# Output projection: two pairs of token tiles per pass instead of one

## The chip, the cores and the metric

The kernel runs on one core of a Trainium2 chip. The metric is the time of one execution on the device in microseconds (us); the median of three runs before is 1721.08 us (1716.45 to 1728.96). Engines are named as in the profile: PE (matrix products), PEld (loading of its stationary operand), DVE (VectorE), ACT (ScalarE), POOL (GpSimd) and SP (here it only issues transfers). Each engine works through its own list in order.

## The reference, cut to what matters

One layer over 2048 tokens of 1024 features: modulated RMSNorm, one input projection, a pooling group and a gated recurrence with 8 heads ("the mixers"), and an output projection. Only the last part matters here:

```python
y = jnp.concatenate([pool_out, hgrn_out], axis=-1) @ w_out[l]     # (2048, 2048) @ (2048, 1024)
h_res = h_res + gate * rms_norm(y, norm_post_w[l])
```

Both mixer groups give 1024 of the 2048 columns that enter `w_out`. All is float32; a product of two float32 matrices is made of three passes in a rounded format (hi times hi, hi times lo, lo times hi), where `lo` is the value less its rounded `hi` (`part`, lines 127 to 130: a copy on ACT, a subtraction on DVE).

## The kernel before, in words

Up to about 1356 us the mixers run. They write their outputs to a buffer `mix` in HBM, and W_out's Strassen sums to `wos`. Then comes the output projection, which is all that the change touches.

It does a matrix product in Strassen-Winograd form: 7 products instead of 8 for a 2x2 block product. Its loop (lines 923 to 966) has 16 steps, called granules here: for g = 0 (the pooling group's half of W_out) and then g = 1 (the recurrence's half), 8 pairs `p_` of token tiles of 128 tokens. One granule works as follows.

- `mix_granule` (lines 819 to 845) loads the two tiles (two transfers of 512 KB, line 823) into the single buffer `raw`, forms on POOL the sums S1, S2, S3, S4 (lines 834, 837, 838, 842: four operations on 128x512) and splits each of seven operands by `part` (lines 129, 130) into a tile `m`, one of six buffers of the tag "w". It is called for the next granule before the products of this one.
- `quad` (lines 376 to 407) makes the seven products A11, S1, S2, A12, S3, S4, A22. Each product is 12 matmuls of 128x128 by 128x512 (line 373). Three PSUM banks X, Z, Y take them: A11 and A12 go into X, S1 and S4 into Z, S2, S3 and A22 into Y. Products add up in a bank, and between two that use the same bank its content is read: line 395 reads Y after S2, line 400 after S3, line 403 Z after S4, line 406 Y after A22, line 389 Z after S1 (all on DVE), line 381 and line 940 X (ACT). So the product that is next in a bank waits for a reader on DVE: S2 into Y and S3 into Y have one other product between them (A12), S3 and A22 too (S4).
- For g = 0 the two result tiles `y` (buffers "y", four) go to HBM as `ypart` (line 945). For g = 1 `ypart` is loaded again (line 936) and added (DVE, line 952, four operations per granule), the sum of squares is taken (ACT, line 957), a power on POOL gives the factor (lines 111, 112), DVE scales (line 961, four), x is loaded (line 954) and added on POOL (line 962, four; in the last granule on DVE), and the tile is stored (line 966; in the last granule in halves, line 964).
- `ypart`, x and the raw pieces of W_out (`load_out`, lines 794 to 817: 14 pieces of 512 KB, each split by `part` or lines 811, 812 into S-tiles that all granules of one g share) use one ring of five buffers, tag "px". `load_out` runs at the start of each g; 28 S-tiles hold one g.

The memory comes from pools that are opened and closed like a stack. `ws` (working tiles of the recurrence) is closed before the last pooling step, and `fin` with "px" and "y" takes its place. `wsp` holds the rest of the mixers' small tiles, `og`, `vc`, `hx` and others (made by `short`, line 138), until the end. The last mixer step is `pool_step` for kb = 7; its two `pool_block` calls (lines 532 to 561) end in a DVE multiplication (line 560) and a store of `sg` to `mix` (line 530).

The order on each engine and queue is laid out ahead by a planner that simulates the times: at each point it takes what is ready, earlier code first, and code in `tc.high_priority()` before that. `load_out(0)` and the first `mix_granule` stand in the code before the last `pool_step`.

Of the kernel before, what the change touches and what calls it, by code (L numbers as in the profile page):

```python
# [44 lines left out]
def build(nc, tc, a):  # L45
# [6 lines left out]
    with tc.tile_pool(name="dram", bufs=1, space=DRAM) as dram, \  # L52
# [21 lines left out]
        def raw_tile(name, shape, dt=F32):  # L74
            return big.tile(shape, dt, name=name, tag="raw", bufs=1)
# [56 lines left out]

        wsp_cm = tc.tile_pool(name="wsp", bufs=1)
        wsp = wsp_cm.__enter__()
        ws_cm = tc.tile_pool(name="ws", bufs=1)
        ws = ws_cm.__enter__()

        def short(name, tag, bufs=1, n=BLK, pool=None):
            return (pool or wsp).tile([P, n], F32, name=name, tag=tag, bufs=bufs)


        masks = {0: cp.tile([P, 32], U8, name="mask0"), 1: cp.tile([P, 16], U8, name="mask1")}
        for q in range(4):
# [3 lines left out]
        mt = wsp.tile([P, 64], F32, name="mt", tag="hx", bufs=2)  # L147
        for m in (2, 4, 8, 16):
            n = 64 // m
            mv = mt.rearrange("p (n m) -> p n m", m=m)  # L150
# [57 lines left out]

        ct = cp.tile([P, KB], F32, name="ct")
        load(ct, a["c"][0].rearrange("(p j) -> p j", j=KB))  # L210
        rows = wsp.tile([P, P], F32, name="rows", tag="w0", bufs=2)
# [164 lines left out]
        def quad(W, c12, c21, c22, begin=None, out=False):  # L376

            X, Z, Y = bank("mm"), bank("mm"), bank("mm")
            product(X, W[0], S["A11"], True)
            with tc.high_priority():  # L380
                nc.scalar.copy(c21, X)
            if begin:

                product(X, W[3], S["A12"], False)
                begin()
            product(Z, W[1], S["S1"], True)
            with tc.high_priority():
                if out:
                    nc.vector.tensor_tensor(c22, Z, c21, ALU.add)
                else:  # L390
                    nc.scalar.copy(c22, Z)  # L391
                    nc.gpsimd.tensor_tensor(c22, c22, c21, ALU.add)  # L392
# [99 lines left out]
        def gate_row():  # L492
# [2 lines left out]
            got = []  # L495

            def fetch(j, n):
                t_ = short("adag", "junk")
# [319 lines left out]

        def mix_granule(g, p_):

            raw = raw_tile("mraw", [P, 2, KB, P])
            for i in range(2):
                nc.sync.dma_start(raw[:, i], mix[2 * p_ + i][:, g * KB:(g + 1) * KB])
            A11, A12, A21, A22 = (raw[:, i, h * KH:(h + 1) * KH] for i in range(2) for h in range(2))
            S1 = wsp.tile([P, KH, P], F32, name="S1", tag="hx", bufs=2)

            def put(src):
                w = w_tile("m")
                wv = w.rearrange("p s (k n) -> p s k n", n=P)
                part(wv[:, 0], wv[:, 1], src)  # L830
                return wv

            r = [put(A11)]
            nc.gpsimd.tensor_tensor(S1, A21, A22, ALU.add)  # L834
            r.append(put(S1))

            nc.gpsimd.tensor_tensor(S1, S1, A11, ALU.subtract)
            nc.gpsimd.tensor_tensor(A21, A11, A21, ALU.subtract)
            r.append(put(S1))
            r.append(put(A12))  # L840
            r.append(put(A21))
            nc.gpsimd.tensor_tensor(S1, A12, S1, ALU.subtract)
            r.append(put(S1))
            r.append(put(A22))
            return r


        steps = []
# [40 lines left out]
        for i, step in enumerate(steps):  # L889
# [3 lines left out]
                load_sums()  # L893
            nxt = weights(steps[i + 1]) if 0 < i < len(steps) - 1 else None
            if i == len(steps) - 1:
                nxt = mix_granule(0, 0)
                O = load_out(0)
            if half == 0 and (what == "hv" and n < HEADS - 1 or what == "pool" and n == HEADS - 1):
                beside(second_sums(n), 2)
# [20 lines left out]
                fin_cm = tc.tile_pool(name="fin", bufs=1)  # L920
                fin.append(fin_cm.__enter__())

        todo = [(g, p_) for g in range(2) for p_ in range(T // P // 2)]
        M = nxt
        for i, (g, p_) in enumerate(todo):
            if p_ == 0:
                S.update(load_out(1) if g else O)
            if g and p_ == 0:
                gn = wsp.tile([P, D], F32, name="gnb", tag="x1", bufs=1)
                nc.sync.dma_start(gn, gnrow[0].partition_broadcast(P))  # L930
            nxt = mix_granule(*todo[i + 1]) if i + 1 < len(todo) else None
            y = [fin[0].tile([P, D], F32, name="y", tag="y", bufs=4) for _ in range(2)]
            if g:
                parts = [fin[0].tile([P, D], F32, name="yp", tag="px", bufs=5) for _ in range(2)]
                for t in range(2):
                    nc.sync.dma_start(parts[t], ypart[2 * p_ + t])
            X = quad(M, y[0][:, BLK:], y[1][:, 0:BLK], y[1][:, BLK:], out=True)
            M = nxt
            with tc.high_priority():
                nc.scalar.copy(y[0][:, 0:BLK], X)  # L940
            if g == 0:
                for f in out_sums(1, p_ % 4, p_ // 4):
                    f()
                for t in range(2):
                    nc.sync.dma_start(ypart[2 * p_ + t], y[t])
                continue
            final = i == len(todo) - 1
            for t in range(2):
                ts = slice((2 * p_ + t) * P, (2 * p_ + t + 1) * P)
                for n in (t, 1 - t):  # L950
                    ns = slice(n * BLK, (n + 1) * BLK)
                    nc.vector.tensor_tensor(y[t][:, ns], y[t][:, ns], parts[t][:, ns], ALU.add)
                xt = fin[0].tile([P, D], F32, name="xf", tag="px", bufs=5)
                nc.sync.dma_start(xt, x[ts])
                ss = wsp.tile([P, 1], F32, name="ss1", tag="ss1", bufs=2)
                junk = wsp.tile([P, D], BF16, name="junk", tag="junk", bufs=1)
                nc.scalar.activation(junk, y[t], AF.Square, accum_out=ss)
                rstd_of(ss, 1, 1.0 / D)
                for n in range(2):
                    ns = slice(n * BLK, (n + 1) * BLK)  # L960
                    nc.vector.scalar_tensor_tensor(y[t][:, ns], y[t][:, ns], ss, gn[:, ns], ALU.mult, ALU.mult)  # L961
                    (nc.vector if final else nc.gpsimd).tensor_tensor(y[t][:, ns], y[t][:, ns], xt[:, ns], ALU.add)
                    if final:
                        nc.sync.dma_start(out[ts, ns], y[t][:, ns])
                if not final:
                    nc.sync.dma_start(out[ts], y[t])
        fin_cm.__exit__(None, None, None)
        wsp_cm.__exit__(None, None, None)

# [15 lines left out]
```

## Time and profile before

| what | value |
|---|---|
| median of the runs | 1721.08 us (1716.45 to 1728.96) |
| the profiled execution's own time | 1724.97 us |
| its span | 1723.3 us |
| PE busy | 1599.1 us, 93% |
| DVE busy | 1101.9 us, 64% |
| POOL busy | 694.5 us, 40% |
| ACT busy | 638.3 us, 37% |
| PE with line 373 in the chain that ended last | 38% of the span |
| DMA in that chain | 17% |

The span is the time from the first to the last instruction of one profiled execution; the time of that execution lies 1.7 us above it. A matmul's busy time runs to its modelled end, and matmuls overlap, so PE's share looks fuller than the work is; a stretch is best judged by how many matmuls it holds. Shares are averages over stages with different limits.

### The profile page before, as it was taken

What the parts mean: (1) busy time and instruction counts of PE and PEld (TensorE: products, weight loads), DVE (VectorE), ACT (ScalarE), POOL (GpSimd) and SP (SyncE); (2) the same over time, 40 slices, a digit from 0 to 9 for tenths busy, and PEclk for the clock granted to TensorE, in tenths of its full rate; (3) what the DMA queues carried; (4) which work ended last, traced back from release to release, by engine and by line L of the source; (5) the groups of instructions that cost most, each with busy time, mean ns of one, the idle gap of its engine ahead of it and who ended that gap; (6) DMA issues with size and microseconds to landing.
All of it is one profiled execution on the core that took longest, in us unless ns stands there. A gap on an engine that the chain in (4) does not pass through costs nothing.

```text
span 1723.3 us, 31604 instructions
## 1 busy us (share of the span) xinstructions
PE 1599.1 (93%) x12249; PEld 1278.4 (74%) x12249; DVE 1101.9 (64%) x1763; ACT 638.3 (37%) x1409; POOL 694.5 (40%) x915
## 2 busy tenths in 40 slices
PE   7679999999999999889999999889999899989896
PEld 6557787887877777767788787677888678867775
DVE  5587767586676868765553545353555864587886
ACT  4554344444444453342223132323222432353332
POOL 1375454746455565211221243534021233225664
PEclk8789999999999999999999999999999999999999
DMA  9637476766757676885344567666545652285553
GB/s 358 228 114 241 174 247 205 243 216 221 231 191 233 215 240 195 292 289 182 120 142 163 179 201 229 214 231 216 204 156 171 208 196 110 98 268 171 192 182 128
DMA packets 221476, 348.67 MB, mean 202 GB/s; under 512 B 45009, under 2 KB 152590, under 8 KB 221326
## 3 DMA queue, kind: packets, MB, share of 16 engines
q1 hardware_dynamic: 221240, 346.62, 59.9%
q8 instruction: 97, 1.59, 0.4%
q14 instruction: 53, 0.43, 0.1%
q10 hardware_dynamic: 86, 0.03, 0.0%
HBM read 203.99 MB, written 142.61 MB: 201 GB/s over the span
## 4 chain that ended last, share of the span: by engine, by line
PE 47%; DMA 17%; DVE 12%; POOL 10%; issue 7%; ACT 4%; SPq 1%; POOLq 0%; DVEq 0%; ACTq 0%
PE ps_mm L373 38%; DMA x<-w_out 4%; DMA wraw<-w_in 3%; DMA wos<-x 3%; DVE m L130 2%; DVE w L130 2%; PE ps_lv L655 2%; DVE lo L130 2%; DMA wraw<-wup 1%; POOL wraw L324 1%; DMA ada<-ada_w 1%; PE ps_tp L714 1%; PE ps_o L730 1%; DVE y L961 1%; PE ps_o L732 1%
## 5 line engine op out<-in xcount | busy, mean ns | idle before, releaser
L373 PE MATMUL ps_mm<-hi,w 128*128 128x512 f32 x2304 | 764.6, 404 | 21.7 <-ACT hi L129 5.8
L373 PEld LDWEIGHTS ps_mm<-hi,w 128*128 128x128 f32 x2304 | 437.4, 192 | 119.9 <-ACT hi L129 8.5
L373 PE MATMUL ps_mm<-lo,w 128*128 128x512 f32 x1152 | 463.8, 403 | 13.9 <-DVE lo L130 10.7
L373 PE MATMUL ps_mm<-hi,m 128*128 128x512 f32 x896 | 289.2, 401 | 27.4 <-DVE y L400 9.8
L373 PEld LDWEIGHTS ps_mm<-lo,w 128*128 128x128 f32 x1152 | 220.8, 192 | 64.2 <-DVE lo L130 15.4
L373 PEld LDWEIGHTS ps_mm<-hi,m 128*128 128x128 f32 x896 | 171.3, 192 | 75.8 <-DVE y L400 11.0
L130 DVE TENSOR_TENSOR w<-wraw,w 128x512 fp32r<-128x512 f32 x168 | 142.7, 860 | 91.5 <-ACT w L129 88.1
L373 PE MATMUL ps_mm<-lo,m 128*128 128x512 f32 x448 | 177.9, 397 | 3.5 <-DVE lo L812 3.5
L129 ACT CAST w<-wraw 128x512 fp32r<-128x512 f32 x168 | 100.9, 620 | 196.4 <-DMA wraw<-w_in 52.4
L648 DVE TENSOR_TENSOR qk<-qk,tcn 128x512 f32<-128x512 f32 x192 | 152.8, 804 | 14.9 <-PE ps_lv L669 9.7
L373 PE MATMUL ps_mm<-hi,wpair 128*128 128x512 f32 x384 | 131.6, 402 | 0.8 <-DVE gx L406 0.8
L373 PEld LDWEIGHTS ps_mm<-lo,m 128*128 128x128 f32 x448 | 86.0, 192 | 22.4 <-DVE lo L812 4.2
L111 POOL TENSOR_SCALAR ss<-ss 128x4 f32<-128x4 f32 (+2 forms) x60 | 16.1, 269 | 182.9 <-ACT og L738 81.5
L373 PEld LDWEIGHTS ps_mm<-hi,wpair 128*128 128x128 f32 x384 | 73.0, 191 | 17.7 <-issue 1.6
L373 PE MATMUL ps_mm<-lo,wpair 128*128 128x512 f32 x192 | 76.7, 399 | 0.1
L834 POOL TENSOR_TENSOR S<-mraw 128x512 f32<-128x512 f32 x16 | 24.3, 1516 | 117.8 <-DMA mraw<-mix 113.5
L130 DVE TENSOR_TENSOR m<-mraw,m 128x512 fp32r<-128x512 f32 x64 | 62.8, 988 | 12.9 <-ACT m L129 12.9
L130 DVE TENSOR_TENSOR m<-S,m 128x512 fp32r<-128x512 f32 x48 | 43.7, 910 | 40.4 <-ACT m L129 39.6
L655 PEld LDWEIGHTS ps_lv<-qk 128*32 128x32 f32 x4096 | 45.5, 111 | 31.1 <-issue 23.5
L593 POOL TENSOR_TENSOR tcn<-tcn 128x128 f32<-128x128 f32 (+4 forms) x160 | 64.1, 401 | 7.9
L324 POOL TENSOR_TENSOR wraw<-wraw 128x512 f32<-128x512 f32 x24 | 32.8, 1367 | 82.3 <-DMA wraw<-w_in 33.0
L392 POOL TENSOR_TENSOR vc<-vc,gx 128x512 f32<-128x512 f32 x16 | 24.4, 1525 | 101.6 <-ACT vc L391 101.6
(277 smaller groups left out, 2597.9 us busy)
## 6 DMA issues: line engine op xcount, KB each, us to landing
wsd<-w SPq DMA_DIRECT2D x168, 512.0 KB, 3.0
w<-wsd SPq DMA_DIRECT2D x120, 512.0 KB, 3.5
wpair<-wsd SPq DMA_DIRECT2D x24, 1024.0 KB, 7.4
wraw<-w_in SPq DMA_DIRECT2D x40, 512.0 KB, 6.2
mraw<-mix SPq DMA_DIRECT2D x32, 512.0 KB, 5.2
ada<-ada_w SPq DMA_DIRECT2D x16, 512.0 KB, 8.8
mix<-g SPq DMA_DIRECT2D x32, 256.0 KB
mix<-sg SPq DMA_DIRECT2D x32, 256.0 KB, 3.2
```

The source lines that it names most:

```text
L129: nc.scalar.copy(hi, raw)
L130: nc.vector.tensor_tensor(lo, raw, hi.bitcast(F32), ALU.subtract)
L324: nc.gpsimd.tensor_tensor(B11, B12, B11, ALU.subtract)
L373: nc.tensor.matmul(ps, w[:, a_, k], s[k][b_], start=start and k == a_ == b_ == 0, stop=k == KH - 1 and a_ == 1, skip_group_check=not start)
L392: nc.gpsimd.tensor_tensor(c22, c22, c21, ALU.add)
L593: nc.gpsimd.tensor_tensor(dst, sv[:, :, 0], sv[:, :, 1], ALU.mult)
L648: nc.vector.tensor_tensor(dst, dst, t_, ALU.mult)
L655: nc.tensor.matmul(ps[q * 32:(q + 1) * 32, c * 16:(c + 1) * 16], K[:, t:t + 32], view(Q, t + m, [(2 * m, 16 // m), (1, m)]), start=True, s ...
L714: nc.tensor.transpose(ps[:, c], src[:, c * C:(c + 1) * C], ident)
L730: nc.tensor.matmul(ops[:, c], attn[:, c], v[:, c], start=True, stop=zero)
L732: nc.tensor.matmul(ops[:, c], Q[:, c * C:(c + 1) * C], s_in, start=False, stop=True)
L834: nc.gpsimd.tensor_tensor(S1, A21, A22, ALU.add)
```

## The change

The loop takes two pairs of token tiles at once: 8 steps instead of 16. `mix_granules` loads both pairs (the second into a new buffer "raw2" of `fin`) and makes the operands of both, product by product; the two constant tiles `accs` of the recurrence serve as S1. `two_quads` makes each of the seven products for the first pair (b = 0) and then for the second (b = 1), in six PSUM banks: three of tag "mm", two of "lv", one of "o". The number of matmuls, splits, sums, additions and transfers stays the same. The ring "px" has three buffers instead of five, and in g = 1 one step uses eight tiles of it (four of `ypart`, four of x). The result tiles of b = 1 come from a new pool `fin2`. For that the small tiles of the mixers move to a pool `wsm` of their own, which is closed after the last mixer step, before `fin2` is opened. Only the last pair of token tiles adds x on DVE and stores in halves, as before.

```diff
+        wsm_cm = tc.tile_pool(name="wsm", bufs=1, side="right")
+        wsm = wsm_cm.__enter__()
...
-            return (pool or wsp).tile([P, n], F32, name=name, tag=tag, bufs=bufs)
+            return (pool or wsm).tile([P, n], F32, name=name, tag=tag, bufs=bufs)
...
-                    raw = fin[0].tile([P, 2, BLK], F32, name="oraw", tag="px", bufs=5)
+                    raw = fin[0].tile([P, 2, BLK], F32, name="oraw", tag="px", bufs=3)
...
+        def mix_granules(g, ps_):
+            raws = [raw_tile("mraw", [P, 2, KB, P]), fin[0].tile([P, 2, KB, P], F32, name="mraw2", tag="raw2", bufs=1)]
+            A11, A12, A21, A22 = ([raw[:, i, h * KH:(h + 1) * KH] for raw in raws] for i in range(2) for h in range(2))
+            S1 = [attn for attn, _ in accs]
+            for raw, p_ in zip(raws, ps_):
+                for i in range(2):
+                    nc.sync.dma_start(raw[:, i], mix[2 * p_ + i][:, g * KB:(g + 1) * KB])
...
+            put(A11)
+            each(S1, A21, A22, ALU.add)
+            put(S1)
+            each(S1, S1, A11, ALU.subtract)
+            each(A21, A11, A21, ALU.subtract)
+            put(S1)
+            put(A12)
+            put(A21)
+            each(S1, A12, S1, ALU.subtract)
+            put(S1)
+            put(A22)
...
+        def two_quads(W, ys):
+            X, Z, Y = ([bank("mm"), bank(tag)] for tag in ("lv", "lv", "o"))
+            c12, c21, c22 = ([y[i][:, ns] for y in ys] for i, ns in
+                             ((0, slice(BLK, D)), (1, slice(0, BLK)), (1, slice(BLK, D))))
...
+            for b in products(X, 0, "A11", True):
+                with tc.high_priority():
+                    nc.scalar.copy(c21[b], X[b])
+            for b in products(Z, 1, "S1", True):
+                add(c22[b], Z[b], c21[b])
+            for b in products(Y, 2, "S2", True):
+                add(c12[b], Y[b], c21[b])
+            for b in products(X, 3, "A12", False):
+                with tc.high_priority():
+                    nc.scalar.copy(ys[b][0][:, 0:BLK], X[b])
+            for b in products(Y, 4, "S3", False):
+                add(c22[b], Y[b], c22[b])
+            for b in products(Z, 5, "S4", False):
+                add(c12[b], Z[b], c12[b])
+            for b in products(Y, 6, "A22", False):
+                add(c21[b], Y[b], c21[b])
...
+        wsm_cm.__exit__(None, None, None)
+        fin2_cm = tc.tile_pool(name="fin2", bufs=1)
+        fin2 = fin2_cm.__enter__()
+        todo = [(g, p_) for g in range(2) for p_ in range(0, T // P // 2, 2)]
...
+            ys = [[pool.tile([P, D], F32, name="y", tag="y", bufs=4) for _ in range(2)] for pool in (fin[0], fin2)]
...
+                parts = [fin[0].tile([P, D], F32, name="yp", tag="px", bufs=3) for _ in range(4)]
+                for t in range(4):
+                    nc.sync.dma_start(parts[t], ypart[2 * p0 + t])
+            two_quads(M, ys)
...
+                final = p_ == T // P // 2 - 1
...
+                    xt = fin[0].tile([P, D], F32, name="xf", tag="px", bufs=3)
```

## Rows read from the trace of the kernel before

**Rows 1.** Stretches: length, then busy us (count) of PE, PEld, DVE, ACT, POOL; clock, DMA.

```profile
1356.25:1411.96 55.71, 47.44 (x181) 36.14 (x181) 46.31 (x68) 28.89 (x50) 15.28 (x11) 0.91 0.69 235
1411.96:1508.79 96.83, 95.80 (x421) 78.67 (x420) 46.07 (x61) 28.46 (x49) 26.55 (x20) 1.00 0.28 104
1508.79:1575.36 66.57, 61.20 (x254) 47.74 (x252) 52.19 (x71) 29.78 (x53) 24.09 (x18) 0.97 0.66 220
1575.36:1688.43 113.07, 100.46 (x421) 78.96 (x420) 91.65 (x100) 37.55 (x67) 72.34 (x62) 0.98 0.58 195
1688.43:1713.75 25.32, 21.73 (x85) 16.49 (x83) 18.02 (x25) 5.58 (x10) 11.15 (x12) 0.93 0.30 105
1713.75:1723.30 9.55, 0.00 (x0) 0.00 (x0) 4.00 (x6) 1.15 (x2) 0.74 (x2) 0.76 0.30 111
```

**Rows 2.** The same view, single granules.

```profile
1411.96:1431.00 19.04, 19.04 (x85) 15.77 (x84) 9.12 (x12) 5.22 (x9) 5.59 (x4) 1.00 0.24 91
...
1529.88:1555.38 25.50, 21.60 (x86) 16.75 (x85) 18.12 (x26) 11.03 (x20) 8.63 (x8) 0.93 0.68 222
...
1599.18:1621.47 22.29, 19.65 (x85) 15.61 (x84) 18.27 (x20) 7.28 (x13) 14.14 (x13) 1.00 0.57 192
```

**Rows 3.** Waits from 1575.4 to 1713.8: waiter, awaited; us in total, times, longest.

```profile
PE ps_mm L373 <- DVE y L400: 9.8, 6, 1.9
```

**Rows 4.** DVE in order of time, 1599.18 to 1621.47: start, us for all, line, count.

```profile
1601.28 2.42 DVE L961 SCALAR_TENSOR_TENSOR y<-y,ss,gnb 128x512 f32<-128x512 f32 x2
1603.63 0.68 DVE L400 TENSOR_TENSOR y<-ps_mm,y 128x512 f32<-128x512 f32 x1
```

**Rows 5.** Lines 962, 834, 961, 952, 400: count, ns min/median/max, first and last start.

```profile
L962 POOL TENSOR_TENSOR y<-y,xf x28: 1283/1732/1749, 1557.0 to 1705.0; 128x512 f32<-128x512 f32 x28
...
L834 POOL TENSOR_TENSOR S<-mraw x16: 1282/1289/3082, 1350.2 to 1684.4; 128x512 f32<-128x512 f32 x16
...
L961 DVE SCALAR_TENSOR_TENSOR y<-y,ss,gnb x32: 740/746/1780, 1556.2 to 1718.0; 128x512 f32<-128x512 f32 x32
...
L952 DVE TENSOR_TENSOR y<-y,yp x32: 674/693/1775, 1541.7 to 1714.5; 128x512 f32<-128x512 f32 x32
...
L400 DVE TENSOR_TENSOR y<-ps_mm,y x16: 676/684/692, 1390.8 to 1709.9; 128x512 f32<-128x512 f32 x16
```

**Rows 6.** Stretches as in rows 1, one of 3.4 us.

```profile
1650.50:1653.90 3.40, 3.40 (x9) 2.64 (x8) 3.40 (x5) 0.00 (x0) 0.67 (x1) 0.50 0.60 187
```

**Rows 7.** Stretch 1356.25 to 1392.92, PE's matmuls on the mixers' weights w alone.

```profile
1356.25:1392.92 36.67, 3.99 (x13) 0.86 0.76 257
```

**Rows 8.** Waits of PE from 1356.25 to 1392.92, as in rows 3.

```profile
PE ps_mm L373 <- DVE lo L812: 3.5, 2, 2.8
```

**Rows 9.** DVE in order of time, 1366 to 1400, as in rows 4.

```profile
1366.90 3.08 DVE L130 TENSOR_TENSOR lo<-oraw,hi 128x512 fp32r<-128x512 f32 x5
...
1395.46 0.68 DVE L560 TENSOR_TENSOR sg<-sg,s 128x512 f32<-128x512 f32 x1
```

**Rows 10.** Waits of the queue SP from 1340 to 1412, as in rows 3.

```profile
SPq L805 <- DMA mix<-g: 2.4, 1, 2.4
```

**Rows 11.** SP in order of time, 1337 to 1400: start, us, line, transfer issued, count.

```profile
1351.86 0.89 SPq L805 DMA_DIRECT2D oraw<-w_out  x2
...
1396.17 0.37 SPq L530 DMA_DIRECT2D mix<-sg  x1
```

**Rows 12.** Chain that ended last, 1380 to 1724: start, us, what.

```profile
1565.21 4.18 DMA xf<-x
...
1619.25 4.99 DMA yp<-ypart
```

**Rows 13.** Transfers of line 530, the store to mix.

```profile
DMA to landing us min/median/max: 2.3/3.2/7.2
```

**Rows 14.** Transfers of line 805, raw pieces of W_out.

```profile
DMA to landing us min/median/max: 4.3/5.1/9.8
```

**Rows 15.** DVE at the end, 1713 to 1724, as in rows 4.

```profile
1718.71 1.28 DVE L962 TENSOR_TENSOR y<-y,xf 128x512 f32<-128x512 f32 x2
```

More of the change, by code (lines that the diff above doesn't have):

```diff
@@ L146, in build @@
             nc.vector.tensor_copy(masks[1][qs], ident[qs, qs].rearrange("p (n two) -> p n two", two=2)[:, :, 0])
-        mt = wsp.tile([P, 64], F32, name="mt", tag="hx", bufs=2)
+        mt = wsm.tile([P, 64], F32, name="mt", tag="hx", bufs=2)
         for m in (2, 4, 8, 16):
@@ L210, in build @@
         load(ct, a["c"][0].rearrange("(p j) -> p j", j=KB))
-        rows = wsp.tile([P, P], F32, name="rows", tag="w0", bufs=2)
+        rows = wsm.tile([P, P], F32, name="rows", tag="w0", bufs=2)
         nc.vector.memset(rows, 0.0)
@@ L374, in product, with quad @@
                                      stop=k == KH - 1 and a_ == 1, skip_group_check=not start)
-        def quad(W, c12, c21, c22, begin=None, out=False):
+        def quad(W, c12, c21, c22, begin=None):
             X, Z, Y = bank("mm"), bank("mm"), bank("mm")
@@ L387, in quad @@
             with tc.high_priority():
[L388 to L392, printed above, removed]
+                nc.scalar.copy(c22, Z)
+                nc.gpsimd.tensor_tensor(c22, c22, c21, ALU.add)
             product(Y, W[2], S["S2"], True)
@@ L497, in fetch @@
             def fetch(j, n):
-                t_ = short("adag", "junk")
+                t_ = short("adag", "junk", pool=wsp)
                 nc.sync.dma_start(t_, ada_w[:, j, 2 * D + n * BLK:2 * D + (n + 1) * BLK])
@@ L817, in load_out, with put, each @@
             return r
[L819 to L844, printed above, removed]
-            return r
+        def mix_granules(g, ps_):
[5 more added lines that the diff above has]
+                    nc.sync.dma_start(raw[:, i], mix[2 * p_ + i][:, g * KB:(g + 1) * KB])
+            r = []
+            def put(srcs):
+                ws_ = []
+                for src in srcs:
+                    w = w_tile("m")
+                    wv = w.rearrange("p s (k n) -> p s k n", n=P)
+                    part(wv[:, 0], wv[:, 1], src)
+                    ws_.append(wv)
+                r.append(ws_)
+            def each(dst, a_, b_, op):
+                for d, x_, y_ in zip(dst, a_, b_):
+                    nc.gpsimd.tensor_tensor(d, x_, y_, op)
+            put(A11)
[9 more added lines that the diff above has]
+            put(A22)
+            return r
@@ new lines, in two_quads, with products, add @@
+        def two_quads(W, ys):
+            X, Z, Y = ([bank("mm"), bank(tag)] for tag in ("lv", "lv", "o"))
+            c12, c21, c22 = ([y[i][:, ns] for y in ys] for i, ns in
+                             ((0, slice(BLK, D)), (1, slice(0, BLK)), (1, slice(BLK, D))))
+            def products(ps, i, name, start):
+                for b in range(2):
+                    product(ps[b], W[i][b], S[name], start)
+                    yield b
+            def add(dst, ps, b_):
+                with tc.high_priority():
+                    nc.vector.tensor_tensor(dst, ps, b_, ALU.add)
+            for b in products(X, 0, "A11", True):
[6 more added lines that the diff above has]
+            for b in products(X, 3, "A12", False):
+                with tc.high_priority():
+                    nc.scalar.copy(ys[b][0][:, 0:BLK], X[b])
[5 more added lines that the diff above has]
+                add(c21[b], Y[b], c21[b])
@@ L895, in build @@
             if i == len(steps) - 1:
-                nxt = mix_granule(0, 0)
+                nxt = mix_granules(0, (0, 1))
                 O = load_out(0)
@@ L921, in build @@
                 fin.append(fin_cm.__enter__())
-        todo = [(g, p_) for g in range(2) for p_ in range(T // P // 2)]
+        wsm_cm.__exit__(None, None, None)
+        fin2_cm = tc.tile_pool(name="fin2", bufs=1)
+        fin2 = fin2_cm.__enter__()
+        todo = [(g, p_) for g in range(2) for p_ in range(0, T // P // 2, 2)]
         M = nxt
-        for i, (g, p_) in enumerate(todo):
-            if p_ == 0:
+        for i, (g, p0) in enumerate(todo):
+            if p0 == 0:
                 S.update(load_out(1) if g else O)
-            if g and p_ == 0:
+            if g and p0 == 0:
@@ L929, in build @@
                 gn = wsp.tile([P, D], F32, name="gnb", tag="x1", bufs=1)
                 nc.sync.dma_start(gn, gnrow[0].partition_broadcast(P))
-            nxt = mix_granule(*todo[i + 1]) if i + 1 < len(todo) else None
-            y = [fin[0].tile([P, D], F32, name="y", tag="y", bufs=4) for _ in range(2)]
+            nxt = mix_granules(todo[i + 1][0], (todo[i + 1][1], todo[i + 1][1] + 1)) if i + 1 < len(todo) else None
+            ys = [[pool.tile([P, D], F32, name="y", tag="y", bufs=4) for _ in range(2)] for pool in (fin[0], fin2)]
@@ L933, in build @@
+            parts = []
             if g:
-                parts = [fin[0].tile([P, D], F32, name="yp", tag="px", bufs=5) for _ in range(2)]
-                for t in range(2):
[L936 to L966, printed above, removed]
@@ new lines, in build @@
+                parts = [fin[0].tile([P, D], F32, name="yp", tag="px", bufs=3) for _ in range(4)]
+                for t in range(4):
+                    nc.sync.dma_start(parts[t], ypart[2 * p0 + t])
+            two_quads(M, ys)
+            M = nxt
+            for b in range(2):
+                p_, y = p0 + b, ys[b]
+                if g == 0:
+                    for f in out_sums(1, p_ % 4, p_ // 4):
+                        f()
+                    for t in range(2):
+                        nc.sync.dma_start(ypart[2 * p_ + t], y[t])
+                    continue
+                final = p_ == T // P // 2 - 1
+                for t in range(2):
+                    ts = slice((2 * p_ + t) * P, (2 * p_ + t + 1) * P)
+                    for n in (t, 1 - t):
+                        ns = slice(n * BLK, (n + 1) * BLK)
+                        nc.vector.tensor_tensor(y[t][:, ns], y[t][:, ns], parts[2 * b + t][:, ns], ALU.add)
+                    xt = fin[0].tile([P, D], F32, name="xf", tag="px", bufs=3)
+                    nc.sync.dma_start(xt, x[ts])
+                    ss = wsp.tile([P, 1], F32, name="ss1", tag="ss1", bufs=2)
+                    junk = wsp.tile([P, D], BF16, name="junk", tag="junk", bufs=1)
+                    nc.scalar.activation(junk, y[t], AF.Square, accum_out=ss)
+                    rstd_of(ss, 1, 1.0 / D)
+                    for n in range(2):
+                        ns = slice(n * BLK, (n + 1) * BLK)
+                        nc.vector.scalar_tensor_tensor(y[t][:, ns], y[t][:, ns], ss, gn[:, ns], ALU.mult, ALU.mult)
+                        (nc.vector if final else nc.gpsimd).tensor_tensor(y[t][:, ns], y[t][:, ns], xt[:, ns], ALU.add)
+                        if final:
+                            nc.sync.dma_start(out[ts, ns], y[t][:, ns])
+                    if not final:
+                        nc.sync.dma_start(out[ts], y[t])
@@ L967, in build @@
+        fin2_cm.__exit__(None, None, None)
         fin_cm.__exit__(None, None, None)
```

## The prediction

> **What bounds the kernel now.** I read the stretches of the span first, because PE's busy share flatters it. In the middle of g = 0 a granule of 84 matmuls takes 19.04 us with PE busy throughout [rows 2]: 0.2267 us per matmul, 2.72 us per product of 12. Sixteen granules need 304.6 us at that rate, and the stage from 1356.25 to 1713.75 takes 357.5 us [rows 1]. The surplus of 52.9 us lies unevenly: the first two granules take 55.7 us instead of 38.1 (17.6 over), granules 2 to 6 lose 1.6, granules 7 to 9 take 66.6 instead of 57.1 (9.5 over), and granules 10 to 15 take 113.1 + 25.3 = 138.4 instead of 114.2 (24.2 over). Then 9.55 us follow without PE [rows 1]. The 1356 us before are not touched.
>
> Next I asked what ends PE's waits in g = 1. The longest total is line 400 on DVE, six waits of up to 1.9 us [rows 3]: the product A22 wants bank Y, and Y's reader stands in DVE's list behind two scalings that took 2.42 us together, although it runs 0.68 us itself [rows 4]. Only one other product, 2.72 us, covers that reader. DVE is busy 18.27 of 22.29 us in such a granule [rows 2], far from full by its own work: an operation that needs 0.69 or 0.75 us takes up to 1.78 when POOL works on 128x512, and POOL's take 1.73 instead of 1.28. Line 400, which reads PSUM, never took over 0.692 [rows 5]. So it is lateness on DVE that costs PE its time. After such gaps the granted clock fell to 0.50 (1.2 of 2.4 GHz), in stretches like [rows 6]; one of about 3.4 us costs half of it, 1.7 us, and the mean of 0.93 in granules 8 and 15 [rows 1, 2] tells of one there too.
>
> **The change, part by part.** Matmuls, splits, sums, additions and bytes are the same, so I price only waiting.
>
> *Banks in g = 1.* Between two uses of a bank there are now three other products instead of one (after S3 of b = 0: S3 of b = 1 and both S4), 8.2 us instead of 2.7. A reader that is 2 us late is hidden. What then sets the pace is PE (19.04) or DVE with POOL. Serialised entirely, DVE's 11 additions and splits that touch no PSUM cost 0.60 each (five follow each other in 3.08 us [rows 9]), its 4 scalings 0.67, POOL's 8 large operations 1.28 [rows 5] and its power pairs 1.5: 6.6 + 2.7 + 10.2 + 1.5 = 21.0 us. Overlapped, less. I take 20.2 per granule, the middle being 20.0; the ends are 19.04 and 22.3 (no gain). Pairs 1 to 3 of g = 1: 3 x 40.4 = 121.2 against 138.4, gain 17.2 (4.6 to 24.2).
>
> *Turn from g = 0 to g = 1.* Each of the seven W_out operands now serves two products in a row, so its successor may come 5.4 us later instead of 2.7, and an S-tile set is freed 32.7 us ahead of its next use instead of 16.3. Granules 2 to 7 took 117.9 us, against 114.2: gain 3.0 (0 to 3.7). The first pair of g = 1 took 45.5 us and should take 40.4: gain 5.1 (0 to 7.4). The ring of three works against this: three pieces per landing of about 5.1 us [rows 14] and about 3 us of splitting, 5.4 us for two pieces, just PE's need.
>
> *Start of g = 0.* Kept: the wait of 2.8 us for the first operand [rows 8], 1.7 us at half clock, 4.0 us of the last mixer products in between [rows 7], and 38.1 us of products: 46.6 us against 55.7. New: two loads of 512 KB ahead of W_out's in SP's queue, and a gate. `fin2` can be written only when everything in `wsm` is done. That such a gate is awaited shows at `fin`: its first load waited 2.4 us for the store of a tile of `ws` [rows 10]. The last user of `wsm` is the store of `sg`, issued at 1396.2 [rows 11] right behind line 560 [rows 9], 3.2 us to land [rows 13], so 1399.4. The first c21 of b = 1 lies in `fin2` and frees bank X for A12 of b = 1, the eighth product, which PE reaches at 1356.25 + 2.8 + 1.7 + 4.0 + 7 x 2.72 = 1383.8, some 2 later with the loads. Price 0 to 14 us. I take 6, a little under the middle: the six operations of the last block were late only because W_out's splits kept DVE full, and with three buffers those come in batches with gaps. 52.6 us, gain 3.1 (-5 to 9.1).
>
> *End.* One step needs eight tiles of a ring of three. The last x tile takes the buffer of the first: first x issued when line 952 has freed the second `ypart` tile, about 1.3 us before PE ends; 4.2 us to land [rows 12]; two additions on POOL at 1.28 to 1.73; then the last x, 5.0 us to land [rows 12]; two additions 1.28 and 3.3 us to the end of the span [rows 15]. -1.3 + 4.2 + 3.0 + 0.3 + 5.0 + 1.3 + 3.3 = 15.8 us after PE's end against 9.55: 6.3, taken as 6.5 (3 to 10) for SP's order. In the steady pairs the ring has room: three such transfers in series start when the second `ypart` tile is freed, 36 us into a pair, and the last result is wanted 35 us later, which leaves 10 us.
>
> *Hidden.* Stores and `mix` loads: the second raw tile is freed after 8 of 14 products, so 16 us remain, as before. If the queue SP stands behind a ring tile, that cover goes.
>
> **Sum.** 3.1 + 3.0 + 5.1 + 17.2 - 6.5 = 21.9 us. The profiled execution took 1724.97 us, 3.9 above the median, so it would be 1703.1; from the median of 1721.08 I get **1699 us**.
>
> **Rivals.**
>
> *DVE and POOL set the pace.* Blocking was seen only side by side [rows 5], and a DVE without idle time meets POOL each time. If all is serial and the lists leave some idle time, a pair takes 42 to 45 us, 43.5 in the middle: four pairs 174 us against 183.9, gain 9.9 in g = 1, total 3.1 + 3.0 + 9.9 - 6.5 = 9.5, 1711.6 us. For it: DVE is 82% busy at 22.3 us and would be 96% at 19.04. Against: five of its 20 operations read PSUM and are not slowed. Chance 0.20. The Trainium skill, page "SBUF — State Buffer", section "SBUF: two separate sides", says that POOL and a DVE operation with two SBUF inputs hold a shared port pair in turn, each for its whole instruction, "the other fully blocks"; rows 5 agree (1.78 for 0.69, 1.73 for 1.28, PSUM reads unharmed). By that rule alone 21.0 us per granule would be near a floor, the four pairs 168 us, and the total 1706.
>
> *The gate.* `fin2` opens at 1399 as now and PE stands 14 us instead of 6, with two half-clock stretches after it (3.4): 21.9 - 8 - 3.4 = 10.5, 1710.6 us. For: the planner left line 560 until 1395. Against: it need not. Chance 0.10.
>
> *The ring, on the other side.* Three transfers in series per pair have 10 us to spare at 5 us each; above 8.3 us each the ring sets the pace, and the loads of `mix` wait behind it in SP. At 12 us a pair takes 38.1 + 11 = 49: three pairs 8.8 us over 138.4, the first pair 3.5 over, and two transfers in series at the end cost 14 more. 3.1 + 3.0 - 3.5 - 8.8 - 20.5 = -26.7: 1748 us. For: W_out's pieces took up to 9.8 [rows 14]. Against: loads of this stage in the chain took 4.2 and 5.0 [rows 12]. Chance 0.08.
>
> *It doesn't do what it says.* The planner picks what is ready and may run one pair's products ahead of the other's; stages as before and the longer end: 1727.6 us. Chance 0.06.
>
> *All waits go.* Pairs at 38.1 us, no gate: 9.1 + 3.7 + 7.4 + 24.2 - 3.5 = 40.9, 1680 us. Chance 0.06.
>
> **How the numbers follow.** The forecast has 0.50. 1% is 17.2 us, about what can be told from no change here: below 1703.9 is faster, above 1738.3 slower. The forecast lies below 1703.9 in 0.85 of its cases (0.43), the best case always (0.06), the pace rival in 0.3 (0.06), the gate in 0.2 (0.02): 0.57 faster. Slower: the ring and a bad mix of gate and end, 0.10. The rest, 0.33, is the same. The range of 1684 to 1722 leaves out the ring, the order that doesn't come and half of the best case, under 0.2 with some of the forecast's own edges.
>
> **What would show it.** Right: each steady pair of g = 0 in 38.1 us; pairs of g = 1 near 40, PE's waits for line 400's successor (the second reader of Y) gone, no stretch at clock 0.50 there; DVE busy over 90%; the end 15 to 16 us long with two x loads in series. Wrong: pairs of 43 or more with DVE operations at 1.7 us throughout (pace); a PE gap of over 6 us before the eighth product with ACT's copy waiting for a store (gate); SP waiting for DVE's additions with the `mix` loads behind (ring). The prediction fails most likely at 20.2 or at the gate.

## The result and the profile after

The changed kernel takes 1703.9 us in the median of four runs, the kernel before 1725.0 us in four runs beside it (the 1721.1 us above is the median of the first three of them); the ratio is 0.988, 95% interval 0.985 to 0.991. Six more runs beside later experiments gave 1701.6 us and 0.986 (0.984 to 0.989). The profiled execution has a span of 1702.4 us, 20.9 less than before.

Stretches of the profile after, cut at the first product of each of the eight steps and at PE's end; columns as in [rows 1]:

```profile
1363.86:1407.60 43.74, 40.17 (x169) 32.68 (x169) 38.79 (x56) 24.40 (x44) 13.29 (x7) 0.92 0.69 223
1407.60:1445.68 38.08, 38.08 (x170) 31.54 (x168) 24.81 (x29) 12.53 (x22) 18.08 (x13) 1.00 0.41 159
1445.68:1483.76 38.08, 38.08 (x170) 31.54 (x168) 18.35 (x24) 10.65 (x18) 10.61 (x9) 1.00 0.29 111
1483.76:1521.84 38.08, 38.08 (x170) 31.54 (x168) 31.68 (x44) 24.91 (x43) 9.00 (x7) 1.00 0.67 223
1521.84:1559.92 38.08, 38.08 (x170) 31.54 (x168) 29.61 (x37) 13.45 (x24) 16.06 (x12) 1.00 0.55 178
1559.92:1598.92 39.00, 38.35 (x169) 31.46 (x168) 34.99 (x39) 13.43 (x25) 27.66 (x22) 1.00 0.54 192
1598.92:1644.58 45.66, 41.10 (x169) 33.14 (x168) 39.31 (x43) 15.50 (x29) 32.18 (x28) 0.93 0.57 197
1644.58:1687.04 42.46, 39.85 (x169) 32.25 (x167) 35.09 (x41) 12.22 (x22) 22.05 (x20) 0.96 0.47 159
1687.04:1702.40 15.36, 0.00 (x0) 0.00 (x0) 10.91 (x12) 2.84 (x6) 8.91 (x10) 0.56 0.67 240
```

Steps 2 to 5 run at PE's rate without a gap, 38.08 us each; before, the eight granules that do the same work took 163.4 us instead of 152.3 [rows 1, 2]. The last three steps, which have to finish the result as well, take 39.0, 45.7 and 42.5. The end without PE grows from 9.55 [rows 1] to 15.4 us. By stage, before less after:

| stage | before | after | gain | predicted |
|---|---|---|---|---|
| until the end of the second granule, or first step | 1411.96 | 1407.60 | 4.4 | 3.1 |
| granules 2 to 7 | 117.9 | 114.2 | 3.7 | 3.0 |
| granules 8 and 9 | 45.5 | 38.1 | 7.4 | 5.1 |
| granules 10 to 15 | 138.4 | 127.1 | 11.3 | 17.2 |
| after PE's end | 9.55 | 15.4 | -5.8 | -6.5 |
| sum | | | 20.9 | 21.9 |

The first line includes the mixers, whose time varies between executions: the first product of the output projection came at 1363.9 and 1367.8 us in two profiles of this same kernel. A fairer count starts at the same matmul in every trace, the 1700th from the end, which still belongs to the mixers (it starts at 1300.6 us before and at 1302.3 after). From there to the end of the second granule, or first step, it is 111.4 us before and 105.3 after (105.4 in the second profile), so this stage gained 6.1 us rather than 4.4; against run 5, whose kernel has the code of the one before in this stage and took 108.9, it gained 3.6. From here on I compare stretches that start at a product.

PE's waits after, from 1363.86 to 1687.04 (columns as in [rows 3]):

```profile
PE ps_mm L375 <- DVE y L868: 6.2, 2, 3.6
PE ps_mm L375 <- DVE lo L811: 3.6, 1, 3.6
PE ps_mm L375 <- ACT hi L810: 1.8, 1, 1.8
PE ps_lv L375 <- DVE m L130: 0.9, 1, 0.9
PE ps_mm L375 <- ACT y L879: 0.6, 1, 0.6
```

Line 868 is what lines 389 to 406 were, the additions from PSUM. Instead of six waits of up to 1.9 us for the addition after S3 [rows 3] there are two, of 3.6 and 2.6 us, in steps 7 and 8, both for the addition after S2, which frees bank Y for S3 of b = 0. The first of them, with DVE's list ahead of it, then PE (start, us, line):

```profile
1612.43 1.42 DVE L1005 SCALAR_TENSOR_TENSOR y<-y,ss,gnb 128x512 f32<-128x512 f32 x2 [1.69 <-POOL ss L112]
1614.29 3.49 DVE L1005 SCALAR_TENSOR_TENSOR y<-y,ss,gnb 128x512 f32<-128x512 f32 x2 [0.44 <-POOL ss L112]
1617.70 1.77 DVE L130 TENSOR_TENSOR m<-mraw,m 128x512 fp32r<-128x512 f32 x1
1619.40 0.68 DVE L868 TENSOR_TENSOR y<-ps_mm,y 128x512 f32<-128x512 f32 x1
...
1623.23 1.75 DVE L1005 SCALAR_TENSOR_TENSOR y<-y,ss,gnb 128x512 f32<-128x512 f32 x1
1624.90 0.68 DVE L868 TENSOR_TENSOR y<-ps_mm,y 128x512 f32<-128x512 f32 x1
```

```profile
1625.73 0.76 PE L375 MATMUL ps_mm<-hi,m 128*128 128x512 f32 x1 [3.61 <-DVE y L868]
```

The addition at 1619.40 takes S1's product, which PE had finished at about 1607; the one at 1624.90 takes S2's, finished at 1612.5, and it is the one that PE waits for. Each runs 0.68 us and stands behind scalings that waited for POOL and of which several then took 1.75 us each instead of 0.75. The cover of 8.2 us is used up, because DVE is not two but twelve microseconds late. PE also ran at half clock from the last 1.5 us of the gap on:

```profile
1624.20:1630.90 6.70, 5.17 (x12) 4.12 (x13) 5.08 (x7) 0.00 (x0) 1.50 (x2) 0.50 0.65 216
```

### The profile page after: what moved, and what is told of

It is laid out like the page before. It is cut to its first block, busy times and chain, and to the rows that moved or that the text cites. A ratio compares the mean times of both kernels' runs of the same rounds, so it can differ in the third digit from the quotient of the medians.

```text
span 1702.4 us, 31635 instructions
## 1 busy us (share of the span) xinstructions
PE 1587.3 (93%) x12249; PEld 1277.0 (75%) x12249; DVE 1113.7 (65%) x1763; ACT 637.3 (37%) x1409; POOL 699.8 (41%) x915
## 4 chain that ended last, share of the span: by engine, by line
PE 51%; DMA 17%; DVE 11%; POOL 9%; issue 4%; ACT 3%; SPq 1%; DVEq 0%; POOLq 0%; ACTq 0%
PE ps_mm L375 36%; DMA x<-w_out 4%; PE ps_lv L375 4%; DMA wraw<-w_in 3%; DMA wos<-x 3%; PE ps_o L375 3%; DVE w L130 2%; PE ps_lv L654 2%; DMA adag<-ada_w 1%; DMA wraw<-wup 1%; DVE y L1005 1%; DMA sum<-hsd 1%; PE ps_tp L713 1%; PE ps_o L729 1%; DVE lo L130 1%
## 5 line engine op out<-in xcount | busy, mean ns | idle before, releaser
L647 DVE TENSOR_TENSOR qk<-qk,tcn 128x512 f32<-128x512 f32 x192 | 151.5, 798 | 15.4 <-PE ps_lv L668 10.3
L375 PE MATMUL ps_mm<-hi,m 128*128 128x512 f32 x448 | 150.6, 398 | 8.7 <-DVE y L868 6.2
L375 PEld LDWEIGHTS ps_mm<-hi,m 128*128 128x128 f32 x448 | 86.4, 193 | 28.4 <-issue 7.0
L375 PE MATMUL ps_mm<-lo,m 128*128 128x512 f32 x224 | 89.2, 398 | 3.6 <-DVE lo L811 3.6
L375 PE MATMUL ps_lv<-hi,m 128*128 128x512 f32 x256 | 84.7, 392 | 0.9 <-DVE m L130 0.9
L111 POOL TENSOR_SCALAR ss<-ss 128x4 f32<-128x4 f32 (+2 forms) x60 | 20.6, 344 | 147.5 <-ACT og L737 80.6
L839 POOL TENSOR_TENSOR attn<-mraw 128x512 f32<-128x512 f32 x16 | 23.5, 1467 | 130.0 <-DMA mraw<-mix 127.5
L130 DVE TENSOR_TENSOR m<-mraw,m 128x512 fp32r<-128x512 f32 x64 | 54.3, 851 | 29.4 <-ACT m L129 29.2
L780 ACT ACTIVATE x<-x,vec 128x512 f32<-128x512 f32 x32 | 23.0, 723 | 108.8 <-DMA x<-w_out 108.8
```

Source lines behind the costliest of these rows:

```text
L111: nc.gpsimd.tensor_scalar(ss, ss, inv, EPS, ALU.mult, ALU.add)
L130: nc.vector.tensor_tensor(lo, raw, hi.bitcast(F32), ALU.subtract)
L647: nc.vector.tensor_tensor(dst, dst, t_, ALU.mult)
L780: nc.scalar.activation(t_[:, 2 * h:2 * h + 2], t_[:, 2 * h:2 * h + 2], AF.Copy, scale=out_scale(g, k + h * KH))
L839: nc.gpsimd.tensor_tensor(d, x_, y_, op)
```

## The experiments

Two theories for what the last three steps gain and still lose stood against each other: the *cover* (products between two uses of a bank) and the *pace* of DVE with POOL; a third, the *ring* of three buffers, for the rest and for the end. The rows below are the last three steps as one stretch for each kernel, with columns as before.

**1. Only the last three steps go back to one pair after the other.**

```diff
+        def apart(g, p0):
+            return g == 1 and p0 > 0
...
-            two_quads(M, ys)
+            if apart(g, p0):
+                banks = [[bank("mm"), bank(tag)] for tag in ("lv", "lv", "o")]
+                two_quads(M, ys, (0,), banks)
+                two_quads(M, ys, (1,), banks)
+            else:
+                two_quads(M, ys)
```

Left out here: `mix_granules` makes the operands of these steps in that order too.

> In the last three steps of g = 1 the two pairs of token tiles are still loaded together and keep their six banks, but all seven products of the first pair run before those of the second, so one other product lies between two uses of a bank instead of three. Theory 1 (cover: the gain there came from the three products between two uses): these three steps, 127.1 us together in the changed kernel, go back towards the 138.4 of the kernel before, 134 to 139; the run takes 1711 to 1716 us. Rival (pace: DVE with POOL sets these steps, whatever the order of products): 125 to 129, and 1702 to 1706 us.

```profile
1562.32:1695.59 133.27, 119.57 (x505) 94.63 (x503) 103.06 (x123) 42.99 (x77) 81.92 (x71) 0.99 0.54 186
```

1707.5 us, ratio 0.992 (0.988 to 0.995). The steps take 6.2 us more than 127.1, a little less than theory 1 said, and PE waits ten times, 13.7 us in all, for line 868's equivalent, so the cover is worth something. The total is only about 4 us longer, which neither theory said (and the two intervals overlap): the end falls to 11.3 us, since now only one pair's tiles are left over after PE's last product. The interleaving pays for its cover with a longer end. The 5 us between these 133.3 and the 138.4 of the kernel before may be the spread of executions or come from what is left of the change here (both pairs loaded together, banks of its own for each pair); no run tells which.

**2. All eight steps so.**

> All eight steps run the first pair's seven products before the second's. Theory 1 (cover in g = 1, and at the two starts of a g the operand of W_out that serves two products in a row): the first step takes 50 to 56 us from its first product instead of 43.7, the turn from g = 0 to g = 1 loses 8 to 11 us, the last three steps as in the run with these alone; 1722 to 1732 us, no faster than the kernel before. Rival (the starts gain because two pairs are loaded at once, not by the order): only the last three steps change, 1711 to 1716 us.

1723.9 us, ratio 0.999 (0.997 to 1.002): the gain is gone. The first step and the turn, in this kernel's profile:

```profile
1369.95:1420.61 50.66, 42.97 (x168) 33.39 (x169) 41.00 (x59) 26.23 (x46) 13.04 (x9) 0.90 0.68 223
...
1534.85:1577.04 42.19, 39.36 (x170) 31.21 (x168) 32.86 (x46) 20.98 (x38) 14.86 (x13) 1.00 0.54 188
```

50.7 instead of 43.7 and 42.2 instead of 38.1: both pairs are loaded together here, and it did not help; the order does. What PE waits for differs between the two places. In the first step it is W_out's splits alone, 8.4 us against 5.4 in the changed kernel, which fits an operand that serves two products in a row. At the turn no operand of W_out is waited for, only readers of banks (line 892 is line 868 there) and splits of the pairs' own operands (tile `m`):

```profile
PE ps_o L375 <- DVE y L892: 0.9, 1, 0.9
PE ps_o L375 <- DVE m L130: 0.8, 1, 0.8
PE ps_mm L375 <- DVE y L892: 0.7, 1, 0.7
PE ps_lv L375 <- ACT m L129: 0.5, 1, 0.5
```

Steps 2 to 4 stay at 38.08. The forecast of 8 to 11 us at the turn was too high, 4.1 came. The last three steps take 134.2 us together, close to run 1, and the end 13.2.

**3. x in a ring of its own.**

```diff
-xt = fin[0].tile([P, D], F32, name="xf", tag="px", bufs=3)
+xt = fin2.tile([P, D], F32, name="xf", tag="xf", bufs=2)
```

> The tiles for x get a ring of two buffers of their own in fin2; the ring of three serves ypart and the pieces of W_out alone. Theory 2 (the shared ring of three delays the fourth ypart tile and the x tiles, and the lateness runs through ACT and DVE to PE): the third and fourth step of g = 1, 45.7 and 42.5 us, fall to 38 to 41, and the end after the last product from 15.4 to 10 to 13; 1690 to 1697 us. Rival (pace): the steps stay at 44 to 46 and 41 to 43, only the end shortens by 2 to 4; 1699 to 1702 us.

```profile
1563.36:1689.50 126.14, 117.12 (x505) 95.28 (x503) 105.91 (x121) 40.42 (x73) 85.06 (x69) 0.99 0.54 183
1689.50:1708.63 19.13, 0.00 (x0) 0.00 (x0) 10.67 (x13) 3.45 (x6) 6.57 (x9) 0.57 0.46 164
```

1710.7 us, ratio 0.993 (0.991 to 0.996), above both ranges. The steps lie within the spread of the changed kernel's two profiles (127.1 and 122.6, run 9), so the shared ring does not cost them anything that can be seen; the ring theory falls there. The end got longer by 3.8, which the rival had not foreseen either: two buffers for x hold the last tiles back more than three shared ones. In the chain that ended last, the transfer of the last x tile now stands after PE's end (1689.50), behind an addition of x on DVE:

```profile
1698.24 0.68 DVE y L1006
...
1699.74 4.24 DMA xf<-x
```

**4. The additions of x on DVE instead of POOL.**

```diff
-(nc.vector if final else nc.gpsimd).tensor_tensor(y[t][:, ns], y[t][:, ns], xt[:, ns], ALU.add)
+nc.vector.tensor_tensor(y[t][:, ns], y[t][:, ns], xt[:, ns], ALU.add)
```

> All additions of x move from POOL to DVE: 28 operations of 128x512 less on POOL, 28 more on DVE. Theory 2 (ring): the buffers come free about 1 us earlier each; the two slow steps lose 1 to 3 us; 1700 to 1703 us. Rival (pace: each operation on POOL blocks DVE for about 1.1 us, so DVE does better by spending 0.6 itself): both slow steps fall to 38 to 41 and DVE's operations with two SBUF inputs run at 0.7 far more often; 1692 to 1697 us. Third possibility: DVE's longer list makes its readers of PSUM later, the steps grow to 46 to 48, 1706 to 1712 us.

```profile
1561.69:1680.61 118.92, 116.52 (x505) 95.39 (x503) 104.40 (x146) 40.69 (x74) 46.61 (x43) 0.99 0.57 198
```

1697.8 us, ratio 0.986 (0.984 to 0.988). DVE runs 25 operations more and is busy 104.4 us instead of 109.4; the steps take 8.2 us less. That is the pace theory's sign, though one of the two slow steps stays at 41.8 us and the total 0.8 above its range. Measured again (runs 9 and 10), the steps differ by 2.8 us.

**5. The same edit on the kernel before**, one pair at a time.

> The kernel before, one pair at a time, with the additions of x on DVE instead of POOL. Pace theory alone (POOL's operations slow DVE, and that made the waits; the order of products does not matter): granules 10 to 15, 138.4 us together, fall to 117 to 123, as in the changed kernel with this edit (119.0 for the last six); 1702 to 1708 us. Cover theory (a reader on DVE is late whenever other work stands before it, and one product of 2.72 us does not cover that): granules 10 to 15 keep 128 to 138, since DVE's list grows; 1714 to 1724 us.

```profile
1578.18:1715.65 137.47, 123.36 (x505) 98.36 (x503) 102.59 (x147) 41.61 (x74) 45.66 (x47) 0.95 0.50 172
```

1727.0 us, ratio 1.002 (0.999 to 1.004). Relief on POOL alone gives nothing: 137.5 us against 138.4, just under the upper end that the cover theory expected, and a total 3 us above its range. PE waits 12.7 us here for line 395, the addition after S2, instead of 9.8 for line 400. So neither theory stands alone; the two parts work together (table in the next section).

**6. POOL adds 128 of each 512 columns.**

```diff
+part_ = ns if final else slice(n * BLK, n * BLK + P)
-(nc.vector if final else nc.gpsimd).tensor_tensor(y[t][:, ns], y[t][:, ns], xt[:, ns], ALU.add)
+(nc.vector if final else nc.gpsimd).tensor_tensor(y[t][:, part_], y[t][:, part_], xt[:, part_], ALU.add)
```

> The changed kernel; on POOL only 128 of each 512 columns of x are added (the rest of that addition is left out, except in the last pair of token tiles); transfers, rings and all else stay. Pace theory: POOL holds back DVE for a quarter of the time in these operations, so the last three steps, 127.1 us, fall to 115 to 119, PE's rate; 1690 to 1695 us. Ring or order theory: the x tiles come free about 1 us sooner each, the steps lose 1 to 4 us in all; 1699 to 1703 us.

```profile
1568.15:1682.56 114.41, 114.41 (x505) 94.41 (x503) 90.54 (x121) 42.10 (x74) 60.43 (x69) 1.00 0.58 205
```

1693.8 us, ratio 0.980 (0.975 to 0.986). DVE's work is unchanged and takes 90.5 us instead of 109.4; PE never stops in these steps and never falls to half clock. Rings, transfers and orders stayed, so with three products between two uses of a bank POOL's additions of x are enough to explain what kept the last three steps from PE's rate.

**7. As 4, and the last step's x in the raw buffers**, which are free by then.

```diff
-xt = fin[0].tile([P, D], F32, name="xf", tag="px", bufs=3)
+if p0 == T // P // 2 - 2:
+    if t == 0:
+        late = raw_tile("xl", [P, 2, D]) if b == 0 else \
+            fin[0].tile([P, 2, D], F32, name="xl2", tag="raw2", bufs=1)
+    xt = late[:, t]
+else:
+    xt = fin[0].tile([P, D], F32, name="xf", tag="px", bufs=3)
```

> The changed kernel with the additions of x on DVE, and the last step's four x tiles in the two raw buffers, which are free by then, instead of in the ring of three. Theory for the end (two x transfers in series after the last product, because the last x waits for the first one's buffer): the end falls from 14.8 to 9 to 11 us and the steps stay near 119; 1691 to 1695 us. Rival (DVE's own list of additions and scalings of four tiles sets the end, 16 operations of about 0.65 us): 13 to 15 us, 1696 to 1699 us.

1694.4 us, ratio 0.982 (0.978 to 0.986). The end is 13.5 us instead of 14.8, as the rival said: without the ring's buffers to wait for, the finishing of three tiles fills it. The total lies in the other theory's range, but it can't decide between them, since the mixers alone vary by more than the two ranges differ.

**8. As 7, with W_out's pieces asked for first.**

```diff
+                O = load_out(0)
                 nxt = mix_granules(0, (0, 1))
-                O = load_out(0)
```

> As the run before this one, with the pieces of W_out asked for ahead of the first two pairs' tiles. Theory (the first step starts late because two loads of 1 MB stand before the first pieces of W_out in the queue): the first product starts 2 to 4 us earlier against the last mixer product and the wait inside it goes; the first step falls from 44 to 45 us to 40 to 42, 1688 to 1692 us. Rival (the pieces wait for the closing of ws, and their splitting on ACT and DVE sets the pace): the same start within 1 us, or later because the tiles come late; 1692 to 1697 us.

1700.8 us, ratio 0.985 (0.981 to 0.989). The first step ends 49.6 us after the start of the mixers' last matmul instead of 45.9 in run 7: worse. The first product does start earlier, even more than the theory said, 2.9 us ahead of that matmul instead of 2.2 behind it; but PE then waits 4.0 us for a split whose sum on POOL had waited for the tiles of `mix`, so they come late, as the rival's second half said. The total lies above both ranges.

**9 to 11. The changed kernel and kernel 4 again, and kernel 4 with only the last step's pairs one after the other** (the condition of 1 for the last p0 alone), side by side.

> The changed kernel as it is, once more, beside the next two on the same chip: 1702 to 1706 us, steps and end as in its first profile (the last three steps 125 to 129 us, end 15 to 16) if these are the program's and not that execution's.

> The changed kernel with the additions of x on DVE, once more, to be compared with the one before on the same chip: 5 to 9 us less than it, all of it in the last three steps.

> As the run before, but in the last step alone the first pair's seven products run before the second's. Theory for the end (three tiles' additions, powers and scalings on DVE and POOL stand behind the last product, because both pairs finish together): the end falls from 14.8 to 9 to 11 us, the last step grows by 0 to 4 for the shorter cover; 1692 to 1697 us against 1696 to 1699 for the run before. Rival (the transfers of x in series): the end stays at 13 to 15, and the total rises by the last step's growth, 1698 to 1702 us.

The three gave 1701.6 us, 0.986 (0.984 to 0.989); 1698.4 us, 0.985 (0.982 to 0.988); 1695.6 us, 0.983 (0.980 to 0.986). The last three steps took 122.6, 119.8 and 120.5 us, so the changed kernel's own vary by 4.5 between executions and its first profile was the slower; its total and its steps came out just below what was expected. The expected 5 to 9 us between 9 and 10 was 3.2 in the medians and 2.8 in the steps. The end of the third:

```profile
1674.47:1686.12 11.65, 0.00 (x0) 0.00 (x0) 7.63 (x12) 1.35 (x4) 2.51 (x4) 0.62 0.63 225
```

11.7 instead of 14.7 us, a little above the forecast, while the last step takes 42.4 (42.1 in run 10, 39.1 in run 4): the end is the finishing of tiles. This version has the lowest median of those that do all the work beside the one in 7; its interval meets that of the changed kernel, so it beats the kernel before clearly and the changed one only by what its stages show. Counted from the 1700th matmul from the end to the end of the span, which leaves the mixers out, its profiled execution took 390.4 us, kernel 4 took 392.5 and 392.2, the changed kernel 400.1 and 395.8, and the kernel before 422.7.

## Why the prediction was right

The sum was 21.9 us and 20.9 came. That closeness is partly luck: the banks in g = 1 gave 5.9 us less than forecast, and the start, the turn and the end 5.0 us more. The direction and the largest part of the mechanism, the cover between two uses of a bank, held. By the line of 1% that the prediction drew, the median of 1703.9 us lies just at the edge of what it called faster.

**Start and gate.** I priced the gate of `fin2` at 6 us between 0 and 14. It cost PE nothing. The store of `sg` was issued at 1383.2, not at 1396, and the copy of c21 for b = 1, the first writer of `fin2`, ran 11.3 us after the one for b = 0 (1376.5), which fits the gate, but just in time; first ACT, then PE after:

```profile
1387.80 0.58 ACT L872 COPY y<-ps_lv 128x512 f32<-128x512 f32 x1
```

```profile
1388.24 0.39 PE L375 MATMUL ps_mm<-hi,m 128*128 128x512 f32 x1
1388.47 0.47 PE L375 MATMUL ps_lv<-hi,m 128*128 128x512 f32 x1
```

The copy ended at 1388.38 and the product A12 of b = 1 began at 1388.47 with no gap; the margin was 0.1 us. The gain of 4.4 (6.1 counted from the same matmul) is nevertheless not far from my 3.1, because the first product began later than I assumed (1363.9), behind the last mixer product instead of ahead of it; PE waited 1.8 and 3.6 us for W_out's splits, and 6.8 us, part of them in the second wait, went by at half clock. Errors of both signs met here.

**Turn.** The size was somewhat low, 3.7 and 7.4 us against 3.0 and 5.1, and the reason was not the one I gave. I priced the operand of W_out that serves two products in a row. PE's waits before, in granules 7 to 9 (1508.79 to 1575.36), name no operand of W_out:

```profile
PE ps_mm L373 <- DVE y L395: 4.2, 3, 2.7
PE ps_mm L373 <- ACT m L129: 1.2, 1, 1.2
```

The longest was for the addition after S2, which stood in DVE's list behind a split that had waited 3.5 us for its copy on ACT:

```profile
1549.08 1.21 DVE L130 TENSOR_TENSOR m<-S,m 128x512 fp32r<-128x512 f32 x1 [3.49 <-ACT m L129]
1550.21 0.68 DVE L395 TENSOR_TENSOR y<-ps_mm,y 128x512 f32<-128x512 f32 x1
```

After, PE does not wait at the turn at all. So it is the same cover as in the banks of g = 1, and I had left it out of this term; run 2 shows that the order makes 4.1 of the 7.4 us, and its waits there are of the same kind.

**Banks in g = 1.** This is the term that was mis-sized: 20.2 us per granule, measured 21.2 (20.4 in the second execution). I had taken a reader to be 2 us late, which 8.2 us of cover hide, and the sharing of DVE and POOL as a matter of pace alone; but when the finishing of one step met the splits of the next, DVE was twelve us late, and PE waited again. Two signs that I had named for being right did not come: there were two stretches at clock 0.50 in g = 1 (6.8 and 3.4 us), and DVE was busy 86% of the last three steps, not over 90%. The runs lay it out, last three steps in us:

| | x added on POOL | x added on DVE | POOL adds a quarter |
|---|---|---|---|
| one pair at a time | 138.4 (before); 133.3 and 134.2 (changed kernel, runs 1 and 2) | 137.5 (kernel before, run 5) | not run |
| product by product | 127.1 and 122.6 | 118.9 and 119.8 | 114.4 |

Against the kernel before, relief without cover gains 0.9 us, the change without relief 11 to 16, and both about 19. The order alone, with loading and banks as changed, is worth 6 to 12 of these (first column, runs 1 and 2 against the second row).

**The pace rival** named the cause of the rest with 1711.6 us, a size too dark for the whole: its 43.5 us per pair were about right for two of the last three steps (45.7 and 42.5; the three average 42.4, in the second execution 40.9, between my 40.4 and its 43.5), while the first step of g = 1 ran at 38.08, since no finished pair stands behind it yet. Blocking is seen as before: scalings on DVE at 1.75 instead of 0.75 above, and 18.9 us of DVE time gone in run 6 for work that is not DVE's. The Trainium skill's rule that I weighed ("SBUF — State Buffer", "SBUF: two separate sides", the shared port pair held in turn) fits these rows. As a floor of 21.0 us per granule it was not borne out: 19.5 in the step of 39.0 us, which held all 16 large operations of POOL and 39 of the 40 on DVE.

**End.** 15.4 us against 15.8 forecast, and my reason was wrong, so the size was luck. I had two transfers of x in series; run 7, with x on DVE, removes them and gains 1.3. The chain that ended last, after:

```profile
1686.41 2.50 POOL y L1006 x2
1688.91 0.08 issue
1689.00 0.52 POOL ss L111
1689.52 0.07 issue
1689.59 0.55 POOL ss L112
1690.14 0.09 issue
1690.23 0.75 POOL ss L111
...
1691.07 0.94 POOL ss L112
1692.01 0.02 issue
1692.03 2.13 DVE y L1005 x2
```

No transfer is in it. Three of the four tiles are scaled only after PE's last product (1687.04), because both pairs' A22 come last, and their additions, powers and scalings stand in line on POOL and DVE; before, it was one tile.

**The ring as a slower case** did not happen and run 3 shows no cost in the steps. That the planner would not keep the order did not happen either: from the second step on, the products come in the order written, and in the first the matmuls of the two pairs alternate in part.

What stays open: how much of the 11 to 16 us the common loading and the separate banks give beside the order; and how much of POOL's effect is the blocking of DVE's operations and how much that the powers of line 112 stand behind POOL's additions, for which DVE's scalings wait. Run 6 removes both.

## What to carry to other kernels

A wait for a reader of a bank has two remedies, more products in between and less work ahead of the reader, and one of them may do next to nothing without the other: here the second gave 0.9 us alone, the whole change 11 to 16, of which the order alone 6 to 12, and both together about 19. Before interleaving two units of work, look at what is finished last: interleaving hides waits inside and lengthens the end, here by 3 to 4 us, which undoing it in the last step alone gave back. And when a term of a sum comes out, look at what the engine waited for all the same: the turn gained what was forecast, and more, by another way.

## What the runs showed of the hardware

The power on POOL, 128x1, took 0.55 us every time before; after, its median is 0.94. Stretch 1560 to 1690 before, then after:

```profile
L112 POOL TENSOR_TENSOR ss<-ss,mhalf x12: 550/550/560, 1566.8 to 1689.6; 128x1 f32<-128x1 f32 x12
```

```profile
L112 POOL TENSOR_TENSOR ss<-ss,mhalf x13: 542/938/1002, 1569.0 to 1689.6; 128x1 f32<-128x1 f32 x13
```

I had expected only the large operations to be slowed by each other. How busy DVE is does not explain it alone: in the last three steps of run 2, with DVE busy 79% of the time, the median is 0.55, in run 5, with 75%, it is 0.88 (1560 to 1690). What stands beside each power no run separates.

A short gap can be followed by half clock or not: before, a wait of 1.89 us (PE goes on at 1649.00) was followed by the stretch of 3.4 us at 0.50 in [rows 6], while waits of 1.85 us (to 1604.36) and 1.87 us (to 1626.67) were not followed by any.

DVE's addition of x costs it 0.82 us on average (run 4, 1560 to 1645) and spares it more than that: 104.4 us busy with it instead of 109.4, and 103.8 instead of 107.4 in runs 10 and 9.
